# A hybrid encoder on one core: attention traced as generators between weight groups, gate jobs moved late, the first two odd jobs in one loop

## The chip, the cores and the metric

The kernel runs on one core of a Trainium2 chip. The metric is device time in microseconds of one execution, the median of several runs; a profile shows one further execution, instruction by instruction.

## The reference, cut to what matters

Sequence 256, width 2048, 16 heads of 128, batch 1, all float32. One even layer, one odd layer, a final RMS norm.

```python
# even layer
u = rms_norm(h, ln_even_g)
qa, ka, va, qb, kb, vb, gate = split(u @ w_in_even)           # 2048 x 6656
ya = gqa_attention(rope(rms_norm(qa)), rope(rms_norm(ka)), va)      # 8 heads (A), 2 key/value heads
yb = diff_attention(qb1, qb2, kb1, kb2, vb, lam, slopes)            # 8 heads (B), two softmaxes each
yb = rms_norm(yb, b_subln_g) * (1 - lambda_init)
h = h + (concat(ya, yb) * silu(gate)) @ w_out_even
# odd layer
qc, kc, vc, gate = split(rms_norm(h, ln_odd_g) @ w_in_odd)     # 2048 x 8192
yc = dilated_window_attention_mix(qc, kc, vc)                       # 16 heads (C)
h = h + (yc * silu(gate)) @ w_out_odd
return rms_norm(h, final_norm_g)
```

## The kernel before

**Weights.** Almost all of TensorE's work is the four projections. They are cut into jobs of 512 output columns. A job has 8 weight groups (`wgroup`, L135) of 1024 values per partition. SP loads a group into `raw` (three buffers), ACT rounds it to `hi` (L151), DVE takes the rest, `lo` (L152); `hi` and `lo` have three buffers each. A product is three matmuls (`mm3`, L157, its lines L159 to L161): hi by hi, hi by lo, lo by hi. A group is 12 matmuls of 512 columns: two token tiles, two slices of the contraction, three products. The activation side (`u`, `y`) is also kept as hi and lo. A job's two sums lie in two of the four `acc` banks until ACT or DVE has read them.

**Order.** The program is traced once, in Python; a scheduler then lays the instructions in each engine's queue by its own estimate of when they are ready, with trace order as priority. The weight splits L151 and L152 are traced at high priority. After that each queue runs in order on the chip.

**Moving a tile to the other layout.** `turned` (L246) transposes 128x512 in 32x32 blocks on DVE (two instructions, L250), and four DMAs of POOL's queue (L254) move the blocks between partitions into a tile `pt`. The reader of `pt` is most often a split (hi on ACT, lo on DVE) ahead of a matmul. `turned_pe` (L257) does the same with four TensorE transposes (L262) and is used for the last group of B heads alone.

**Even layer (L537 to L559).** Job kv, then for each of two groups of heads: q of A, gate of A, gate of B, q of B, k of B, v of B. Behind the gate of A the four A heads are traced (scores L335 to L337, softmax L343 to L348, `turned`, `weights`, `weighted_v` L361, which multiplies by the gate at L367 and splits into `y`). Behind k of B the softmaxes of four B heads are traced (`softmax_b`, L390), behind v the rest (`pair_b`, L411, with the gate in L430). So the last B heads of the second group stand at the very end of the layer, behind its last projection job.

**Output projections.** `jobs_out` (L182) runs the first two jobs in one loop: weight groups 0 to 5 of both, then groups 6 and 7 of both; groups 6 and 7 read `y[12]` to `y[15]`, which are finished last. After each even output job DVE adds the residual, and `turned` with `times_turned` builds the next layer's `u`.

**Odd layer (L578 to L602).** Four times: gate, q, k, v; the softmaxes of four heads behind k, the weighted sums behind v.

Of the kernel before, what the change touches and what calls it, by code (L numbers as in the profile page):

```python
# [17 lines left out]
P = 128  # L18
# [46 lines left out]
def job_columns(name):  # L65

    if name == "even":
        cols = [(A_KV0, 512)]
        for c in (0, 512):
            cols += [(b + c, 512) for b in (0, GATE_E, GATE_E + 1024, B_Q0, B_K0, B_V0)]  # L70
        return cols
    if name == "odd":
        return [(b * D + c, 512) for c in range(0, D, 512) for b in (3, 0, 1, 2)]
    return list(CHUNKS_E if name == "out_even" else CHUNKS)
# [19 lines left out]
def trunk(ctx, tc, x, xt, w_even, w_oe, w_odd, w_oo, gain_cols, rows, final_g, rope_c, geo_c, out):  # L94
# [24 lines left out]
    ones = work.tile([P, 512], F32, tag="x", name="ones", bufs=2)[:, :P]  # L119
    G.memset(ones, 1.0)  # L120
    ident = const.tile([P, P], F32, name="ident")
    make_identity(nc, ident)
# [10 lines left out]
    loads, splits = [], []  # L133

    def wgroup(wb, c0, wd, kg, into=None, pieces=1, beside=None):  # L135
        w, where = wb
        kn = 1024 // wd
        raw = wpool.tile([P, 1024], F32, tag="raw", name="raw", bufs=3)
        if into is None:
            hi = wpool.tile([P, kn, wd], F32R, tag="hi", name="hi")  # L140
            lo = wpool.tile([P, kn, wd], F32R, tag="lo", name="lo")
        else:
            hi, lo = into
        rv = raw.rearrange("p (k c) -> p k c", k=kn)
        n = kn // pieces
        for i in range(pieces):
            ks = slice(i * n, (i + 1) * n)
            cs = slice(i * n * wd, (i + 1) * n * wd)
            loads.append(nc.sync.dma_start(raw[:, cs], w[where[c0] + kg][:, cs]))
            with tc.high_priority():  # L150
                A.activation(hi[:, ks], rv[:, ks], AF.Copy)  # L151
# [3 lines left out]
        return hi, lo  # L155

# [9 lines left out]
    def job_steps(ps, w, c0, wd, a, kgs, beside=None, pieces=lambda kg: 1):  # L166
        kn = 1024 // wd
        for kg in kgs:
            hi, lo = wgroup(w, c0, wd, kg, pieces=pieces(kg), beside=beside)
            for t in range(NT):  # L170
                for kk in range(kn):
                    k = kg * kn + kk
                    ts = slice(t * P, (t + 1) * P)
                    mm3(ps[t], a[k][:, 0, ts], a[k][:, 1, ts], hi[:, kk], lo[:, kk], k == 0, k == NK - 1)

# [6 lines left out]
    def jobs_out(w, chunks, a):  # L182

        (c0, wd), (c1, _) = chunks[:2]
        ps = [job_banks(wd) for _ in range(2)]
        for kgs in (range(6), range(6, 8)):
            for p, c in zip(ps, (c0, c1)):
                job_steps(p, w, c, wd, a, kgs)
        for i, (c, wd) in enumerate(chunks):
            yield i, slice(c, c + wd), ps[i] if i < 2 else job_t(w, c, wd, a)  # L190
# [4 lines left out]
    u = [ug[k // UG][:, k % UG] for k in range(NK)]  # L195

    def make_u(k, src, gain):

        A.activation(u[k][:, 0], src, AF.Copy, scale=gain)  # L199
        V.scalar_tensor_tensor(u[k][:, 1], src, gain, f(u[k][:, 0]), op0=ALU.mult, op1=ALU.subtract)  # L200
# [45 lines left out]
    def turned(src):  # L246

        x = work.tile([P, 4, 4, 32], F32, tag="x", name="x", bufs=2)
# [7 lines left out]

    def turned_pe(src):  # L257

        ps = att.tile([P, 512], F32, tag="att", name="tp").rearrange("p (n k) -> p n k", n=4)
        for j in range(2):  # L260
            for t in range(NT):
                T.transpose(ps[:, 2 * j + t], src[:, t, j * P:(j + 1) * P], ident)  # L262
        return ps.rearrange("p n (a c) -> p n a c", a=4)
# [18 lines left out]
    def pair_t(z, pair, tag, bufs=2):  # L282

        ps = turned(cols(z, pair))
# [6 lines left out]
    def pair_q64(z, pair):  # L291
        ps = turned(cols(z, pair))
# [7 lines left out]
    def pair_k64(z, pair):  # L300
        ps = turned(cols(z, pair))
# [59 lines left out]
    def weighted_v(h, p, v, vs, gate):  # L361
        ph, pl = weights(p)
        o = bank()[:, :S]
# [46 lines left out]
    def pair_b(h, ps, v, zg, turned):  # L410

        os = []
        ss = small.tile([P, 8], F32, tag="ss8", name="ss4", bufs=2)[:, :2 * NT]
        for j in range(2):
            ph, pl = weights(ps[j])
# [10 lines left out]
        yt = stile()  # L426
        for j in range(2):
            c = slice(j * HD, j * HD + HD)
            for t in range(NT):
                V.scalar_tensor_tensor(yt[:, t, c], os[j][:, t], r[:, 2 * j + t:2 * j + t + 1], zg[:, t, c], op0=ALU.mult,  # L430
                                       op1=ALU.mult)
        yt = turned(yt)
        for j in range(2):
            y[h + j] = acts.tile([P, 2, S], F32R, tag="y", name="y")
            times_turned(y[h + j][:, 0], y[h + j][:, 1], yt[:, 2 * j:2 * j + 2], gsub[:, 0:1])
# [100 lines left out]
    k_a = pair_t(tok_heads(ps_kv, 1, 2), 0, "ka", 1)  # L536
    for g in range(2):  # L537
        c = 512 * g
        zq = tok_heads(job_t(w_even, c, 512, u) if g else ps_q0, 0, 4)
        qs = [pair_t(zq, pair, "q") for pair in range(2)]  # L540
        zg = gate_t(job_t(w_even, GATE_E + c, 512, u), rh)
        for pair in range(2):
            gate = turned(cols(zg, pair))
            for j in range(2):
                p = softmax_a(qs[pair][:, :, j], k_a[:, :, g])
                weighted_v(4 * g + 2 * pair + j, p, v_a[:, 0], slice(g * HD, g * HD + HD), gate[:, 2 * j:2 * j + 2])
        zg = gate_t(job_t(w_even, GATE_E + 1024 + c, 512, u), rh)
        zq = evac_t(job_t(w_even, B_Q0 + c, 512, u), rs)
        qs = [pair_q64(zq, pair) for pair in range(2)]
        zk = evac_t(job_t(w_even, B_K0 + c, 512, u), rstd)  # L550
        v = v_tile()
        ps = []
        for pair in range(2):
            kh, kl = pair_k64(zk, pair)
            for j in range(2):
                ps.append(softmax_b(4 * g + 2 * pair + j, qs[pair][:, :, j], kh[:, :, j], kl[:, :, j]))
        evac_v(v, job_t(w_even, B_V0 + c, 512, u), rstd)
        for pair in range(2):
            pair_b(8 + 4 * g + 2 * pair, ps[2 * pair:2 * pair + 2], v[:, pair], cols(zg, pair), turned_pe if g else turned)  # L559


    y_even = list(y)
    un = [acts.tile([P, UG, 2, S], F32R, tag="u", name="u", bufs=NK // UG) for _ in range(NK // UG)]
    u = [un[k // UG][:, k % UG] for k in range(NK)]
    parts_o = small.tile([P, NT, 4], F32, tag="parts4", name="parts4", bufs=1)
    for i, cs, ps in jobs_out(w_oe, CHUNKS_E, y_even):
        for t in range(NT):
            V.tensor_add(tok[:, t, cs], tok[:, t, cs], ps[t])
        for k in range(cs.start // P, cs.stop // P, 2):
            xk = turned(tok[:, :, k * P:k * P + S])  # L570
            for m in range(2):
                src, gain = xk[:, 2 * m:2 * m + 2], gcol[:, NK + k + m:NK + k + m + 1]
                times_turned(u[k + m][:, 0], u[k + m][:, 1], src, gain)
        for t in range(NT):
            square_sum(parts_o[:, t, i:i + 1], tok[:, t, cs])


    for g in range(4):  # L578
# [4 lines left out]
        zg = gate_t(ps, rh)  # L583
        gates = [turned(cols(zg, pair)) for pair in range(2)]
        zq = evac_t(job_t(w_odd, c, 512, u), rs)
        qs = [pair_t(zq, pair, "q") for pair in range(2)]
        zk = evac_t(job_t(w_odd, D + c, 512, u), rstd)
        p = []
        for pair in range(2):
            k = pair_t(zk, pair, "k")  # L590
            p += [softmax_c(4 * g + 2 * pair + j, qs[pair][:, :, j], k[:, :, j]) for j in range(2)]
        v = v_tile()
        evac_v(v, job_t(w_odd, 2 * D + c, 512, u), rstd)
        for pair in range(2):
            for j in range(2):
                weighted_v(4 * g + 2 * pair + j, p[2 * pair + j], v[:, pair], slice(j * HD, j * HD + HD),
                           gates[pair][:, 2 * j:2 * j + 2])
# [80 lines left out]
```

## Time and profile before

| | us |
|---|---|
| median of 3 runs (lowest, highest) | 950.54 (948.35, 951.49) |
| profiled execution, its own time | 952.57 |
| span of its trace | 950.8 |
| PE busy (matmul) | 890.5 (94% of the span) |
| DVE busy | 650.4 (68%) |
| ACT busy | 523.7 (55%) |
| POOL busy | 257.1 (27%) |
| mean granted TensorE clock | 0.964 of full speed |

How to read it: matmuls are pipelined, so a busy PE is not a PE at its peak; what counts is the distance from one matmul's start to the next. The granted clock is full (2.4 GHz) in most of the span and falls to half (1.2 GHz) in parts of one stretch near the middle. Idle time of DVE, ACT and POOL costs nothing as long as PE goes on.

### The profile page before, as it was taken

How to read it: one execution, taken by the hardware profiler on the slowest of the kernel's cores; microseconds unless marked ns; L12 is line 12 of the kernel's file. 1: busy time of each engine (PE TensorE's matmuls, PEld its weight loads, DVE VectorE, ACT ScalarE, POOL GpSimd, SP SyncE). 2: the span in 40 equal slices, each digit the busy share in tenths (PEclk: the TensorE clock that was granted, in tenths of full speed). 3: DMA queues.
4: the chain of work that ended last, by engine and by line, in shares of the span. 5: the costliest groups of instructions: out<-in, count | busy, mean ns of one | idle time of the engine just before them, and what ended most of it. 6: DMA issues, size and time to landing. Idle time of an engine off the chain costs nothing.

```text
span 950.8 us, 12189 instructions
## 1 busy us (share of the span) xinstructions
PE 890.5 (94%) x4124; PEld 742.3 (78%) x4124; DVE 650.4 (68%) x937; ACT 523.7 (55%) x842; POOL 257.1 (27%) x395
## 2 busy tenths in 40 slices
PE   9999999999999666279999999999999999999896
PEld 7788888888888555267888888888888888888686
DVE  6688656787786557537776666767776776676564
ACT  6756655677555436525554455655554565455442
POOL 0023102132231232423121233424332433251200
PEclk9999999999999779569999999999999999999999
DMA  8867666564566434115766656665576657665553
GB/s 295 296 218 236 218 200 210 189 220 166 189 225 216 135 89 166 34 55 165 237 221 218 220 188 212 222 213 194 191 243 214 202 183 226 228 208 183 175 199 133
DMA packets 57662, 186.16 MB, mean 196 GB/s; under 512 B 10688, under 2 KB 11456, under 8 KB 57600
## 3 DMA queue, kind: packets, MB, share of 16 engines
q1 hardware_dynamic: 46656, 162.57, 50.9%
q0 software_dynamic: 10944, 22.83, 8.1%
q8 instruction: 32, 0.52, 0.2%
q14 instruction: 30, 0.25, 0.1%
HBM read 161.50 MB, written 2.10 MB: 172 GB/s over the span
## 4 chain that ended last, share of the span: by engine, by line
PE 56%; DVE 2%; ACT 2%; issue 2%; DMA 2%; POOL 1%; POOLq 0%; DVEq 0%; ACTq 0%
PE acc_t L159 18%; PE acc_t L160 17%; PE acc_t L161 17%; DMA pt<-x 2%; POOL pt L254 1%; PE bank L160 1%; ACT s L346 1%; PE bank L161 1%; PE bank L159 1%; DVE x L250 0%; PE bank L337 0%; PE bank L336 0%; PE bank L335 0%; ACT hi L151 0%; DVE s L381 0%
## 5 line engine op out<-in xcount | busy, mean ns | idle before, releaser
L152 DVE TENSOR_TENSOR lo<-raw,hi 128x1024 fp32r<-128x1024 f32 (+1 forms) x294 | 360.1, 1226 | 197.3 <-ACT hi L151 196.6
L151 ACT ACTIVATE hi<-raw 128x1024 fp32r<-128x1024 f32 (+1 forms) x294 | 309.0, 1053 | 279.0 <-PE acc_t L161 228.0
L160 PE MATMUL acc_t<-lo,u 128*128 128x512 f32 x928 | 360.5, 390 | 0.5 <-DVE lo L152 0.2
L161 PE MATMUL acc_t<-hi,u 128*128 128x512 f32 x928 | 359.9, 390 | 0.0
L159 PE MATMUL acc_t<-hi,u 128*128 128x512 f32 x928 | 330.2, 390 | 0.6 <-ACT u L199 0.6
L254 POOL DMA_DIRECT2D pt<-x x332 | 180.9, 574 | 402.1 <-issue 135.1
L160 PEld LDWEIGHTS acc_t<-lo,u 128*128 128x128 f32 x928 | 174.1, 188 | 37.6 <-DVE lo L152 2.4
L159 PEld LDWEIGHTS acc_t<-hi,u 128*128 128x128 f32 x928 | 174.0, 188 | 37.3 <-ACT u L199 1.6
L161 PEld LDWEIGHTS acc_t<-hi,u 128*128 128x128 f32 x928 | 174.3, 188 | 35.2
L159 PE MATMUL acc_t<-hi,y 128*128 128x512 f32 (+1 forms) x256 | 95.4, 397 | 6.0 <-ACT y L225 4.6
L160 PE MATMUL acc_t<-lo,y 128*128 128x512 f32 (+1 forms) x256 | 100.1, 393 | 0.4 <-DVE lo L152 0.4
L161 PE MATMUL acc_t<-hi,y 128*128 128x512 f32 (+1 forms) x256 | 95.4, 388 | 0.0
L386 POOL TENSOR_SCALAR bias<-geo 128x512 f32<-128x512 f32 x24 | 40.3, 1681 | 166.1 <-DVE s L381 160.6
L159 PEld LDWEIGHTS acc_t<-hi,y 128*128 128x128 f32 x256 | 50.6, 198 | 18.5 <-ACT y L225 6.2
L160 PEld LDWEIGHTS acc_t<-lo,y 128*128 128x128 f32 x256 | 50.6, 198 | 10.1 <-DVE lo L152 1.1
L161 PEld LDWEIGHTS acc_t<-hi,y 128*128 128x128 f32 x256 | 50.3, 197 | 9.4
L346 ACT ACTIVATE s<-s,nm 128x256 f32<-128x256 f32 x64 | 31.9, 499 | 32.3 <-DVE nm L343 31.4
L250 DVE STREAM_TRANSPOSE x<-z 128x256 f32<-128x256 f32 x82 | 46.9, 611 | 3.4 <-DMA pt<-x 3.3
L250 DVE STREAM_TRANSPOSE x<-s 128x256 f32<-128x256 f32 x68 | 39.7, 620 | 3.8 <-ACT s L376 3.4
L225 ACT ACTIVATE ph<-pt 128x512 fp32r<-128x512 f32 x32 | 19.9, 621 | 26.6 <-DMA pt<-x 26.6
L232 ACT ACTIVATE z<-acc_t,rstd 128x512 f32<-128x512 f32 x40 | 26.9, 680 | 7.4 <-PE acc_t L161 5.7
L226 DVE TENSOR_TENSOR pl<-pt,ph 128x512 fp32r<-128x512 f32 x32 | 21.7, 677 | 13.5 <-ACT ph L225 13.5
(140 smaller groups left out, 704.4 us busy)
## 6 DMA issues: line engine op xcount, KB each, us to landing
raw<-in_w_in_odd SPq DMA_DIRECT2D x128, 512.0 KB, 4.1
raw<-in_w_in_even SPq DMA_DIRECT2D x102, 512.0 KB, 4.1
pt<-x POOLq DMA_DIRECT2D x332, 64.0 KB, 3.3
raw<-in_w_out_even SPq DMA_DIRECT2D x32, 512.0 KB, 3.3
raw<-in_w_out_odd SPq DMA_DIRECT2D x32, 512.0 KB, 3.6
tok<-in_x SPq DMA_DIRECT2D x4, 512.0 KB, 8.1
xk<-in_xt SPq DMA_DIRECT2D x6, 256.0 KB, 5.5
raw<-in_w_in_even SPq DMA_DIRECT2D x4, 256.0 KB, 4.4
```

The costliest lines, as they stand in the source:

```text
L151: A.activation(hi[:, ks], rv[:, ks], AF.Copy)
L152: splits.append(V.tensor_sub(lo[:, ks], rv[:, ks], f(hi[:, ks])))
L159: T.matmul(ps, ah, bh, start=start, stop=False)
L160: T.matmul(ps, ah, bl, start=False, stop=False)
L161: T.matmul(ps, al, bh, start=False, stop=stop)
L225: A.activation(hi, src, AF.Copy)
L226: V.tensor_sub(lo, src, f(hi))
L232: A.activation(z[:, t], ps[t], AF.Copy, scale=r[:, t:t + 1])
L250: V.transpose(x[:, :, 2 * m:2 * m + 2].rearrange("p b t c -> p t b c"), src[:, :, m * P:(m + 1) * P].rearrange("p t (r b) -> p t b r", b=4))
L254: G.dma_start(dst[:, a].rearrange("p n c -> p (n c)"), x[32 * a:32 * a + 32].rearrange("r b n c -> r (b n c)"))
L346: A.activation(e[:, t], s[:, t], AF.Exp, bias=nm[:, t:t + 1], accum_out=den[:, t:t + 1])
L386: G.tensor_scalar_mul(b, geo[:, 0], -slope)
```

## The change

1. `tick()` is called after each weight group. Attention steps become generators (`spawn`): each runs up to a `yield n` and goes on n weight groups later. So the pieces of the attention of one job are traced between the weight groups of the next jobs, at distances written by hand (6 to 10 groups from a `turned` to the reader of its tile).
2. `behind()` ties the readers of a moved tile, on ACT and on DVE, behind the split of the weight group that was traced last.
3. Even jobs in a new order: kv, q of A twice, then q, k, v of B, a gate, and again q, k, v of B, and three gates. The gates are no longer needed for the attention: A heads leave an ungated sum in `o` (a copy of ACT), B heads a normalised one in `yt` (ACT); `finish` and `finish_b` multiply by the gate later. The weight blocks lie in memory in the new order.
4. Odd jobs: q, k, v, gate for the first two groups, then q, k, v of the third and fourth, then the last two gates. The first q and k share a loop (`two_jobs`) as the output jobs do.
5. `turned_pe` and the identity are gone; tag `x`, which `turned` writes, has four buffers in place of two. `u` of the next layer is made by `task_u`, five groups after its `turned`.

```diff
-        cols = [(A_KV0, 512)]
-        for c in (0, 512):
-            cols += [(b + c, 512) for b in (0, GATE_E, GATE_E + 1024, B_Q0, B_K0, B_V0)]
-        return cols
+        return [(c, 512) for c in (A_KV0, 0, 512, B_Q0, B_K0, B_V0, GATE_E, B_Q0 + 512, B_K0 + 512, B_V0 + 512,
+                                   GATE_E + 1024, GATE_E + 512, GATE_E + 1536)]
...
+        quads = [(b * D + c, 512) for c in range(0, D, 512) for b in (0, 1, 2, 3)]
+        return quads[:11] + quads[12:15] + quads[11:12] + quads[15:]
...
+    tasks, now = [], [0]
+    def spawn(steps, delay=0):
+        tasks.append([now[0] + delay, steps])
+    def tick():
+        now[0] += 1
+        for task in list(tasks):
+            if task[0] <= now[0]:
+                try:
+                    task[0] = now[0] + next(task[1])
+                except StopIteration:
+                    tasks.remove(task)
...
+    @contextmanager
+    def behind():
+        with tc.issue_after(firsts[-1].ins), tc.issue_after(splits[-1].ins):
+            yield
...
+                    advance(lambda: a[k] is not None)
                     mm3(ps[t], a[k][:, 0, ts], a[k][:, 1, ts], hi[:, kk], lo[:, kk], k == 0, k == NK - 1)
+            tick()
...
+    def weighted_v(o, p, key):
+        yield 6
+        with behind():
+            ph, pl = weights(p)
+        yield 1
+        yield from until(lambda: key in values)
+        v, vs = values[key]
+        ps = bank()[:, :S]
         for kt in range(NT):
-            mm3(o, v[:, kt, 0, vs], v[:, kt, 1, vs], ph[:, kt], pl[:, kt], kt == 0, kt == NT - 1)
-        yf = work.tile([P, S], F32, tag="yf", name="yf")
-        V.tensor_mul(row_quarters(yf), row_quarters(o), gate)
-        y[h] = acts.tile([P, 2, S], F32R, tag="y", name="y")
-        split(y[h][:, 0], y[h][:, 1], yf)
+            mm3(ps, v[:, kt, 0, vs], v[:, kt, 1, vs], ph[:, kt], pl[:, kt], kt == 0, kt == NT - 1)
+        A.copy(o, ps)
+    def finish(h, o, gate):
+        gate = turned(gate)
+        yield 6
+        with behind():
+            V.tensor_mul(quarters(o), quarters(o), gate)
+        for j in range(2):
+            y[h + j] = acts.tile([P, 2, S], F32R, tag="y", name="y")
+            split(y[h + j][:, 0], y[h + j][:, 1], o[:, j])
...
+    def pair_b(i, q, kh, kl, outs):
+        ps = []
+        for j in range(2):
+            ps.append(softmax_b(i + j, q[:, :, j], kh[:, :, j], kl[:, :, j]))
+            yield 2
+        yield 4
+        yield from until(lambda: ("b", i) in values)
...
-                V.scalar_tensor_tensor(yt[:, t, c], os[j][:, t], r[:, 2 * j + t:2 * j + t + 1], zg[:, t, c], op0=ALU.mult,
-                                       op1=ALU.mult)
-        yt = turned(yt)
+                A.activation(yt[:, t, j * HD:(j + 1) * HD], os[j][:, t], AF.Copy, scale=r[:, 2 * j + t:2 * j + t + 1])
+        outs[i // 2] = yt
+    def finish_b(h, i, outs, gate):
+        yield from until(lambda: outs[i] is not None)
+        V.tensor_mul(outs[i], outs[i], gate)
+        yt = turned(outs[i])
+        yield 6
...
+    def task_bk(g, z, qs):
+        ts = [turned(cols(z, pair)) for pair in range(2)]
+        yield 7
+        for pair in range(2):
+            with behind():
+                kh, kl = pair_k64(ts[pair])
+            yield 1
+            spawn(pair_b(4 * g + 2 * pair, qs[pair], kh, kl, ob))
+            yield 4
...
     for g in range(2):
         c = 512 * g
+        spawn(task_bq(evac_t(job_t(w_even, B_Q0 + c, 512, u), rs), qs))
+        spawn(task_bk(g, evac_t(job_t(w_even, B_K0 + c, 512, u), rstd), qs))
+        ps = job_t(w_even, B_V0 + c, 512, u)
...
+        if g:
+            zg = gates(1024)
+            for pair in range(2):
+                spawn(finish_b(8 + 2 * pair, pair, ob, cols(zg, pair)))
+        zg = gates(c)
+        for pair in range(2):
+            spawn(finish(4 * g + 2 * pair, oa[2 * g + pair], cols(zg, pair)))
+    zg = gates(1536)
+    for pair in range(2):
+        spawn(finish_b(12 + 2 * pair, 2 + pair, ob, cols(zg, pair)))
...
     for g in range(4):
         c = 512 * g
-        ps = job_t(w_odd, 3 * D + c, 512, u)
         if g == 0:
+            ps_q, ps_k = two_jobs(w_odd, c, D + c, u)
             rstd, rs, rh = token_stats(parts_o, 1.0 / math.sqrt(HD))
...
+        if g < 2:
+            gates(g)
+    gates(2)
+    gates(3)
```

## Rows read from the trace of the kernel before

**Rows 1.** Stretches of the span: busy us (instructions) of each engine, granted clock.
```profile
core 0: us, PE busy (x) PEld busy (x) DVE busy (x) ACT busy (x) POOL busy (x), PEclk, DMA share, GB/s
220.00:300.00 80.00, 80.00 (x389) 67.40 (x388) 64.63 (x102) 48.52 (x89) 25.12 (x37) 1.00 0.60 198
300.00:440.00 140.00, 93.29 (x389) 75.41 (x388) 80.77 (x139) 63.38 (x137) 40.73 (x63) 0.78 0.32 102
0.00:431.00 431.00, 382.69 (x1722) 316.58 (x1723) 294.68 (x461) 244.43 (x429) 105.85 (x166) 0.93 0.56 185
440.00:860.00 420.00, 420.00 (x1926) 350.37 (x1925) 295.76 (x388) 235.15 (x339) 136.16 (x205) 1.00 0.65 214
874.00:896.00 22.00, 18.70 (x78) 14.88 (x77) 11.75 (x19) 9.43 (x17) 6.53 (x12) 0.92 0.66 215
```

**Rows 2.** Chain that ended last, about 440 us: start, us, what.
```profile
438.32 0.45 PE acc_t L159 x2
441.04 0.45 PE acc_t L159 x2
```

**Rows 3.** Timeline of PE: start, us, engine, line, operation, tiles, shape.
```profile
307.52 0.28 PE L335 MATMUL bank<-ka,q 128*128 128x256 f32 x1
308.72 0.28 PE L161 MATMUL bank<-ph,va 128*128 128x256 f32 x1
```

**Rows 4.** PE's instructions by form in 300 to 440: count, busy, mean, idle before.
```profile
L160 PE MATMUL acc_t<-lo,y 128*128 128x512 f32 x75 | 32.9, 439 | 0.4 <-DVE lo L152 0.4
L398 PE MATMUL bank<-kh,q 128*128 128x256 f32 x16 | 5.2, 369 | 17.6 <-ACT kh L307 17.6
L160 PE MATMUL bank<-v,ph 128*128 128x128 f32 x16 | 5.1, 319 | 0.0
L160 PE MATMUL acc_t<-lo,u 128*128 128x512 f32 x12 | 4.7, 389 | 0.0
L159 PE MATMUL bank<-ph,va 128*128 128x256 f32 x8 | 3.3, 415 | 12.4 <-ACT ph L225 12.4
L262 PE MATMUL tp<-ident,s 128*128 128x128 f32 x8 | 2.6, 453 | 11.3 <-DVE s L430 11.3
L337 PE MATMUL bank<-ka,q 128*128 128x256 f32 x6 | 2.2, 371 | 0.0
```

**Rows 5.** Chain that ended last, 370 to 412 and 872 to 900.
```profile
377.06 3.81 DMA pt<-x
...
882.07 5.88 DMA pt<-x
```

**Rows 6.** PE's instructions by form in 874 to 896.
```profile
L160 PE MATMUL bank<-pl,v 128*128 128x256 f32 x4 | 1.6, 390 | 0.3 <-DVE pl L226 0.3
```

**Rows 7.** All waits: engine, line, waited for; us in total, times, longest.
```profile
ACT hi L151 <- PE acc_t L161: 228.0, 178, 6.8
ACT ph L225 <- DMA pt<-x: 26.6, 13, 5.4
PE acc_t L159 <- ACT y L225: 4.6, 4, 1.5
```

**Rows 8.** Groups of instructions over the span: count, busy us, mean ns.
```profile
L152 DVE TENSOR_TENSOR lo<-raw,hi 128x1024 fp32r<-128x1024 f32 (+1 forms) x294 | 360.1, 1226 | 197.3 <-ACT hi L151 196.6
L250 DVE STREAM_TRANSPOSE x<-s 128x256 f32<-128x256 f32 x68 | 39.7, 620 | 3.8 <-ACT s L376 3.4
L343 DVE TENSOR_REDUCE nm<-s 128x2 f32<-128x512 f32 x32 | 21.5, 681 | 0.4
L381 DVE TENSOR_TENSOR s<-bank,bias 128x512 f32<-128x512 f32 x32 | 21.5, 680 | 6.8 <-PE bank L399 4.7 <-POOL bias L388 0.7 <-POOL bias L386 0.6
L346 ACT ACTIVATE s<-bank,nm 128x256 f32<-128x256 f32 x16 | 7.4, 471 | 9.4 <-DVE nm L343 9.4
```

**Rows 9.** Line L254, POOL's DMA issues: ns min/median/max; then DMA to landing.
```profile
L254 POOL DMA_DIRECT2D pt<-x x332: 534/569/752, 57.9 to 882.1; - x166
...
DMA to landing us min/median/max: 2.0/3.3/6.7
```

More of the change, by code (lines that the diff above doesn't have):

```diff
@@ L1 @@
 import math
-from contextlib import ExitStack, nullcontext
+from contextlib import ExitStack, contextmanager
 import numpy as np
@@ L8 @@
 from concourse import mybir
-from concourse.masks import make_identity
 F32 = mybir.dt.float32
@@ L130, in trunk @@
         T.matmul(idle[:, :P], ones, ones, start=True, stop=True)
-    loads, splits = [], []
+    loads, firsts, splits = [], [], []
     def wgroup(wb, c0, wd, kg, into=None, pieces=1, beside=None):
@@ L194, in trunk @@
     ug = [acts.tile([P, UG, 2, S], F32R, tag="u", name="u", bufs=NK // UG) for _ in range(NK // UG)]
-    u = [ug[k // UG][:, k % UG] for k in range(NK)]
+    u = [None] * NK
     def make_u(k, src, gain):
+        u[k] = ug[k // UG][:, k % UG]
         A.activation(u[k][:, 0], src, AF.Copy, scale=gain)
@@ L246, in turned @@
     def turned(src):
-        x = work.tile([P, 4, 4, 32], F32, tag="x", name="x", bufs=2)
+        x = work.tile([P, 4, 4, 32], F32, tag="x", name="x", bufs=4)
         for m in range(2):
@@ L535, in trunk, with task_ka, head_a, task_a @@
     evac_v(v_a, ps_kv, rstd, 256)
-    k_a = pair_t(tok_heads(ps_kv, 1, 2), 0, "ka", 1)
+    keys_a = []
+    def task_ka(z):
+        ps = turned(z)
+        yield 8
+        with behind():
+            keys_a.append(pair_t(ps, "ka", 1))
+    oa, ob = [out_pair() for _ in range(4)], [None] * 4
+    def head_a(o, q, k, key):
+        yield from weighted_v(o, softmax_a(q, k), key)
+    def task_a(g, z):
+        qs = [turned(cols(z, pair)) for pair in range(2)]
+        yield 10
+        for pair in range(2):
+            with behind():
+                q = pair_t(qs[pair], "q")
+            yield 1
+            for j in range(2):
+                spawn(head_a(oa[2 * g + pair][:, j], q[:, :, j], keys_a[0][:, :, g], ("a", g)), 2 * j)
+            yield 3
@@ new lines, in task_bq @@
+    def task_bq(z, qs):
+        ts = [turned(cols(z, pair)) for pair in range(2)]
+        yield 8
+        for pair in range(2):
+            with behind():
+                qs.append(pair_q64(ts[pair]))
+    def task_bk(g, z, qs):
+        ts = [turned(cols(z, pair)) for pair in range(2)]
+        yield 7
+        for pair in range(2):
+            with behind():
+                kh, kl = pair_k64(ts[pair])
+            yield 1
+            spawn(pair_b(4 * g + 2 * pair, qs[pair], kh, kl, ob))
+            yield 4
@@ L537, in trunk, with gates @@
+    for g in range(2):
+        values["a", g] = v_a[:, 0], slice(g * HD, g * HD + HD)
+    spawn(task_ka(tok_heads(ps_kv, 1, 2)))
+    spawn(task_a(0, tok_heads(ps_q0, 0, 4)))
+    spawn(task_a(1, tok_heads(job_t(w_even, 512, 512, u), 0, 4)))
+    def gates(c):
+        return gate_t(job_t(w_even, GATE_E + c, 512, u), rh)
     for g in range(2):
         c = 512 * g
-        zq = tok_heads(job_t(w_even, c, 512, u) if g else ps_q0, 0, 4)
-        qs = [pair_t(zq, pair, "q") for pair in range(2)]
@@ L562, in trunk @@
[L562 to L565 removed]
+        qs = []
+        spawn(task_bq(evac_t(job_t(w_even, B_Q0 + c, 512, u), rs), qs))
+        spawn(task_bk(g, evac_t(job_t(w_even, B_K0 + c, 512, u), rstd), qs))
+        ps = job_t(w_even, B_V0 + c, 512, u)
+        v = v_tile()
+        evac_v(v, ps, rstd)
@@ new lines, in trunk @@
+        for pair in range(2):
+            values["b", 4 * g + 2 * pair] = v[:, pair]
+        if g:
[3 more added lines that the diff above has]
+        zg = gates(c)
+        for pair in range(2):
+            spawn(finish(4 * g + 2 * pair, oa[2 * g + pair], cols(zg, pair)))
+    zg = gates(1536)
+    for pair in range(2):
+        spawn(finish_b(12 + 2 * pair, 2 + pair, ob, cols(zg, pair)))
+    y_even = y
@@ new lines, in trunk, with task_u @@
+    ug = [acts.tile([P, UG, 2, S], F32R, tag="u", name="u", bufs=NK // UG) for _ in range(NK // UG)]
+    parts_o = small.tile([P, NT, 4], F32, tag="parts4", name="parts4", bufs=1)
+    def task_u(cs):
+        ks = range(cs.start // P, cs.stop // P, 2)
+        xs = [turned(tok[:, :, k * P:k * P + S]) for k in ks]
+        yield 5
+        for k, x in zip(ks, xs):
+            for m in range(2):
+                un[k + m] = ug[(k + m) // UG][:, (k + m) % UG]
+                with behind():
+                    times_turned(un[k + m][:, 0], un[k + m][:, 1], x[:, 2 * m:2 * m + 2],
+                                 gcol[:, NK + k + m:NK + k + m + 1])
@@ L568, in trunk @@
             V.tensor_add(tok[:, t, cs], tok[:, t, cs], ps[t])
[L569 to L573, printed above, removed]
+        spawn(task_u(cs))
         for t in range(NT):
             square_sum(parts_o[:, t, i:i + 1], tok[:, t, cs])
+    u = un
+    y = [None] * NK
@@ new lines, in trunk, with gates, head_c, task_q @@
+    oc = []
+    def gates(g):
+        zg = gate_t(job_t(w_odd, 3 * D + 512 * g, 512, u), rh)
+        for pair in range(2):
+            spawn(finish(4 * g + 2 * pair, oc[2 * g + pair], cols(zg, pair)))
+    def head_c(h, o, q, k):
+        yield from weighted_v(o, softmax_c(h, q, k), ("c", h))
+    def task_q(z, qs):
+        ts = [turned(cols(z, pair)) for pair in range(2)]
+        yield 7
+        for pair in range(2):
+            with behind():
+                qs.append(pair_t(ts[pair], "q"))
@@ L578, in trunk, with task_k @@
+    def task_k(g, z, qs):
+        ts = [turned(cols(z, pair)) for pair in range(2)]
+        yield 6
+        for pair in range(2):
+            with behind():
+                k = pair_t(ts[pair], "k")
+            yield 1
+            for j in range(2):
+                h = 4 * g + 2 * pair + j
+                spawn(head_c(h, oc[2 * g + pair][:, j], qs[pair][:, :, j], k[:, :, j]), 2 * j)
+            yield 3
     for g in range(4):
         c = 512 * g
-        ps = job_t(w_odd, 3 * D + c, 512, u)
@@ L592, in trunk @@
-        v = v_tile()
[L593 to L597, printed above, removed]
+        else:
+            ps_q, ps_k = job_t(w_odd, c, 512, u), None
+        qs = []
+        oc += [out_pair() for _ in range(2)]
+        spawn(task_q(evac_t(ps_q, rs), qs))
+        spawn(task_k(g, evac_t(ps_k or job_t(w_odd, D + c, 512, u), rstd), qs), 1)
@@ L600, in trunk @@
+        ps = job_t(w_odd, 2 * D + c, 512, u)
+        v = v_tile()
+        evac_v(v, ps, rstd)
+        for i in range(4):
+            values["c", 4 * g + i] = v[:, i // 2], slice(i % 2 * HD, i % 2 * HD + HD)
+        if g < 2:
+            gates(g)
+    gates(2)
+    gates(3)
     parts = small.tile([P, NT, 5], F32, tag="parts5", name="parts5", bufs=1)
```

82 lines of the change are left out of this document (27 added, 55 removed).

## The prediction, made before the changed kernel ran

> **What bounds the kernel now.** I read the stretches of the span first, for PE's instruction count and the granted clock; then the chain that ended last, for the pace of an undisturbed matmul; then the waits and the groups of instructions, for what would be next.
>
> From 440 to 860 PE is busy without a gap at full clock [rows 1]. Its pace there is that of the weight groups: the chain shows the same matmul pair of one group and of the next 2.72 us apart, 438.32 and 441.04 [rows 2]. A group is 12 matmuls of 512 columns, so one is 2.72 / 12 = 0.2267 us. ACT rounds each group and then waits for PE to give a buffer back, 228.0 us in 178 waits [rows 7]: the splits run ahead, DVE and ACT are not the bound there. So the odd layer has nothing to give except at its end.
>
> From 300 to 440 it is different. The stretch holds 389 PE instructions, as many as the 80 us from 220 to 300, but takes 140 us, and the clock's mean falls to 0.78 [rows 1]. What PE waits for there is attention of the second head group: `ph` of the A heads (12.4 us), `kh` of the last B pair (17.6 us), the scaled tile of the PE transpose (11.3 us) [rows 4]. The chain shows what these waits are made of: landings of moved tiles, such as 3.81 us at 377.06 [rows 5], each followed by a split, scores, a softmax and the next move. No projection work is left to run beside it but the first output jobs, and their last groups read just these heads. The same at the end of the odd layer, from 874 to 896: 78 instructions in 22 us [rows 1], with a landing of 5.88 us in the chain [rows 5].
>
> **The sum: what the stretches would take at full pace.** From 300 to 440 the forms are: 512 columns, 75 and 12 for each of the three products (two records of one line are missing there, so 259 found); 256 columns, 16 each of two lines (L398, L399), 8 and 6 each of three lines, so 74; 128 columns, 16 each of three lines, and 8 transposes, so 56 [rows 4]. Ten steps of 256 columns take 308.72 - 307.52 = 1.20 us, 0.12 each [rows 3]; I take the same for 128 columns, an upper bound. 259 x 0.2267 + (74 + 56) x 0.12 = 58.7 + 15.6 = 74.3 us. Lost: 140 - 74.3 = 65.7 us. It includes the half clock after each gap, which goes with the gap.
>
> From 874 to 896: 12 of the 78 have 256 columns, 4 each of three lines [rows 6]. 66 x 0.2267 + 12 x 0.12 = 16.4 us; lost: 5.6 us.
>
> **The change, part by part.**
>
> *Order and generators, even layer.* The last projection job is now a gate, and two more gates stand ahead of it. The B heads of the second group are traced from 7 groups after job k of B on, and end some 24 groups after it, at the end of the second of the three gates. Behind the last job there remain only evacuation, tanh, a product, one move and one split. For that, the output loop offers 12 groups, 12 x 2.72 = 32.6 us, ahead of the first reader of `y[12]`. The move itself: two transposes at 0.620 [rows 8], four issues at 0.569, landing 3.3 [rows 9], together 6.8 us; with the longest values 1.24 + 3.0 + 6.7 = 10.9 us. With six groups (16.3 us) of written delay the split is still well ahead. So the whole 65.7 us go, and the 8 TensorE transposes with them (1.0 us): -66.7.
>
> *Gates last, odd layer.* The last projection job is a gate here too, and nothing but a product stands behind it: -5.6. If the cover failed, it would cost again what 874 to 896 cost.
>
> *First odd jobs in one loop.* The border of the layers lies behind 440, and from there to 860 PE loses nothing [rows 1]; twice the cover for `u[12]` to `u[15]` is worth 0 here.
>
> *What is added.* 24 copies of a weighted sum on ACT, at most the 0.471 of another PSUM read of that width [rows 8], 11.3 us, and 16 scalings of half that width, at most 7.5 us. DVE loses as many products and gains one of 512 columns for each pair. Eight more DMAs on POOL, 8 x 0.569 = 4.6 us. All of it lies beside PE: with the loss gone, the work from 0 to 431 stands in 431 - 66.7 = 364 us, and then ACT has (244.4 + 18.8) / 364 = 72%, POOL (105.9 + 4.6) / 364 = 30%, DVE 294.7 / 364 = 81% [rows 1]. DVE is the one to look at. But from 220 to 300 it had 64.63 / 80 = 81% and PE lost nothing [rows 1]. So I take 0 for the additions; the other end is the first rival.
>
> *New waits.* Each copy on ACT waits for a weighted sum of PE, and the next L151 is queued behind it. PE needs that split only when the buffered groups are used up, two groups or 5.4 us later. `behind` makes a reader of a moved tile wait behind the newest split, on both engines, and what follows in the queue waits with it. In the trace of before ACT waited 13 times for `pt` of `ph`, 26.6 us in all, at most 5.4 [rows 7]: about the slack of the buffers. With the written delays these waits should vanish. I price them at 0, with the second rival as the other end.
>
> *Joints.* Where an output loop reads its first late `y`, PE waited 4.6 us in 4 places, at most 1.5 [rows 7]. Those in the middle and end stretches are in the sums above; new joints can cost between 0 and 4.6; I take half, +2.3.
>
> Profiled execution: 952.57 - 66.7 - 5.6 + 2.3 = 882.6. The median of before lies 2.0 below its profiled execution, so **880.5** as a median. The start and the tail behind the last matmul stay as they are.
>
> **Rivals.**
>
> *DVE becomes the bound in places* (chance 0.15). For each group of four B heads the softmaxes are traced within 8 weight groups. On DVE a head takes 2 x (0.680 + 0.681) + 2 x 0.620 = 3.96 us [rows 8] without its smaller steps; four heads 15.8, eight splits at 1.226 [rows 8] 9.8, together 25.6 us. PE needs 21.8 + 4 x 8 x 0.12 = 25.6 us for the same. So DVE is full before the small steps, the key splits, the gate products and the moves of neighbouring jobs. If those add a quarter, 6.4 us, at each of three dense places (two B groups, and the rotary work of q of A, now two jobs in a row), and no buffer takes it up, 19 us come back: 878 + 19 = 897, some more with half clock. For it: the count. Against it: the splits have priority, a late softmax delays only itself, and the average is that of a stretch without loss.
>
> *Moved tiles late in the queue: slower than before* (0.04). The diff has 97 `behind` blocks when their loops are run out. If a tile took longer than its delay (6 groups, 16.3 us; 5 groups, 13.6, for `u`) plus the two buffered groups, each block would hold up the splits behind it and PE with them. It decides at about 16.3 + 5.4 = 22 us from transpose to landing, where the rows give 7 to 11, or 13 with two tiles in a row on POOL's queue. To eat up the 72 us, 0.75 us at each block are enough; at 1 us each the time would be 878 + 97 = 975. The rule behind it is in the Trainium skill, "TensorE: Matmul & The Clock Gate", section on the array's architectural detail: ACT and DVE take their queues in strict order, and only PE pulls weight loads ahead. By that rule one late tile stops every split behind it, which speaks against `behind`; the ACT waits on moved tiles named above agree with it. A second rule would lengthen the landing: the Trainium skill, "DMA: Bandwidth & Descriptors", section "SWDGE vs HWDGE vs iDMA", says that DVE can lock GpSimd out of the memory in which it writes its descriptors. The trace does not bear it out: the issues took 534 to 752 ns over the whole span [rows 9], dense DVE stretches included. The sum without it is the one above; with it, this rival.
>
> *Half the tail stays* (0.06). Trace order is only a priority. If the scheduler still puts the second group's B heads late, or the yields are too long for the three gates to cover, about half of 66.7 stays: 878 + 33 = 911.
>
> *It doesn't do what it says* (0.03). The gaps only move to the new joints, for instance because moved tiles find no free slot in their pool. I count at most 21 of its 22 slots in use in trace order, so little speaks for it; the time would be about 950.
>
> **How the numbers follow.** The forecast has 0.72. Its own range is 873 to 889: downwards from 878.2 without joints, less the spread of the three runs (3.1 us) and some 2 us for paces read to 0.01 us over 130 small matmuls; upwards with all of the joints and one dense place. The range with 8 in 10 takes in the first rival: **873 to 900**. A difference within 0.3% (2.9 us) can't be told from none here. Faster: 0.72 + 0.15 + 0.06 = 0.93; same: 0.03; slower: 0.04.
>
> **What would show it.** Right: full granted clock in every stretch up to the tail; no PE gap above 1.5 us between 50 us and the tail; PE's count in any 20 us of the even layer at the full-pace level; ACT's waits on `pt` near 0; the wait of L151 for PE still the largest. Wrong: PE waiting for `lo` (DVE is the bound), L151 behind a late `ph` or `y`, or a gap with `kh`, `ph` or `y` as releaser just ahead of the output loops. What would break the sum most is a scheduler order on PE in which an attention matmul stands ahead of its input on the chip: a gap of the landing's size, followed by half clock, for each.

## The result and the profile after

| | before | after |
|---|---|---|
| median, us (lowest, highest) | 949.79 (948.35, 951.49) | 880.29 (880.15, 880.41) |
| profiled execution / its span | 952.57 / 950.8 | 880.24 / 878.5 |
| PE busy | 890.5 (94%) | 868.3 (99%) |
| DVE / ACT / POOL busy | 68% / 55% / 27% | 74% / 61% / 31% |
| mean granted TensorE clock | 0.964 | 0.997 |

The ratio is 0.9268, 95% interval 0.925 to 0.9285. The forecast was 880.5. PE's busy time fell by 22 us although its work is the same but for eight transposes: matmuls at half clock count as busy for longer (from 300 to 440 the `lo` by `y` product took 439 ns as a mean before [rows 4], 389 after).

The stretches of the kernel after, in the form of [rows 1] (busy us and instructions of each engine, granted clock, DMA):

```profile
core 0: us, PE busy (x) PEld busy (x) DVE busy (x) ACT busy (x) POOL busy (x), PEclk, DMA share, GB/s
60.00:300.00 240.00, 239.50 (x1170) 201.73 (x1169) 204.60 (x310) 173.99 (x332) 93.77 (x137) 1.00 0.61 203
180.00:220.00 40.00, 40.00 (x203) 33.95 (x202) 38.34 (x66) 30.62 (x67) 20.71 (x28) 1.00 0.61 197
300.00:440.00 140.00, 140.00 (x625) 116.13 (x625) 99.73 (x151) 75.54 (x115) 31.27 (x56) 1.00 0.67 221
```

From 300 to 440 PE now runs 625 instructions where it ran 389 [rows 1], at full clock. Of them 612 have 512 columns and 13 have 128, which at the pace of [rows 2, 3] is 140.3 us: no loss is left. All that PE still waits for, in the whole span (engine, line, waited for; us in total, times, longest):

```profile
PE idle L126 <- POOL nhalf L120: 1.0, 1, 1.0
PE acc_t L187 <- DVE lo L148: 0.7, 2, 0.5
PE acc_t L186 <- ACT u L232: 0.3, 1, 0.3
```

No wait for `ph`, `kh` or `y` is left [rows 4]. ACT's waits for moved tiles and for PE, to be set beside [rows 7]:

```profile
ACT hi L147 <- PE acc_t L188: 196.7, 155, 2.7
ACT ph L258 <- DMA pt<-x: 13.5, 11, 2.7
```

The splits still run ahead of PE. In this span the difference is 950.8 - 878.5 = 72.3 us, which is the prediction's 66.7 + 5.6. By place, with the first matmul of the odd layer and the last of the kernel, before and then after:

```profile
476.33 0.62 PE L159 MATMUL acc_t<-hi,u 128*128 128x512 f32 x2
942.46 0.28 PE L161 MATMUL acc_l<-u,y 128*128 128x256 f32 x1
```

```profile
409.75 0.62 PE L186 MATMUL acc_t<-hi,u 128*128 128x512 f32 x2
870.14 0.28 PE L188 MATMUL acc_l<-u,y 128*128 128x256 f32 x1
```

The odd layer starts 66.6 us earlier, and takes 460.4 us from there to the last matmul in place of 466.1: 5.7 less. The place and the size were right. The experiments ask for the cause.

### The profile page after: what moved, and what is told of

The parts are those of the page before. It is cut to its first block, busy times and chain, and to the rows that moved or that the text cites. A ratio compares the mean times of both kernels' runs of the same rounds, so it can differ in the third digit from the quotient of the medians.

```text
span 878.5 us, 12205 instructions
## 1 busy us (share of the span) xinstructions
PE 868.3 (99%) x4116; PEld 728.4 (83%) x4116; DVE 649.0 (74%) x917; ACT 531.8 (61%) x882; POOL 271.0 (31%) x401
## 4 chain that ended last, share of the span: by engine, by line
PE 94%; DMA 2%; DVE 1%; ACT 1%; issue 1%; SPq 0%; POOLq 0%; POOL 0%; DVEq 0%; ACTq 0%
PE acc_t L187 29%; PE acc_t L188 29%; PE acc_t L186 29%; PE bank L187 1%; DMA raw<-in_w_in_even 1%; PE bank L188 1%; PE bank L186 1%; DMA tok<-in_x 1%; PE bank L359 1%; PE bank L358 1%; PE bank L357 1%; DVE lo L148 0%; PE bank L438 0%; PE bank L437 0%; ACT hi L147 0%
## 5 line engine op out<-in xcount | busy, mean ns | idle before, releaser
L287 POOL DMA_DIRECT2D pt<-x x340 | 185.4, 593 | 331.0 <-ACT hi L147 109.4
L188 PE MATMUL acc_t<-hi,y 128*128 128x512 f32 (+1 forms) x256 | 96.1, 376 | 0.0
L187 PE MATMUL acc_t<-lo,y 128*128 128x512 f32 (+1 forms) x256 | 96.1, 376 | 0.0
L186 PE MATMUL acc_t<-hi,y 128*128 128x512 f32 (+1 forms) x256 | 87.0, 376 | 0.0
L425 POOL TENSOR_SCALAR bias<-geo 128x512 f32<-128x512 f32 x24 | 45.7, 1905 | 131.8 <-DVE s L420 124.2
L187 PEld LDWEIGHTS acc_t<-lo,y 128*128 128x128 f32 x256 | 48.2, 188 | 8.8
L186 PEld LDWEIGHTS acc_t<-hi,y 128*128 128x128 f32 x256 | 48.1, 188 | 8.8
L188 PEld LDWEIGHTS acc_t<-hi,y 128*128 128x128 f32 x256 | 48.2, 188 | 8.6
L283 DVE STREAM_TRANSPOSE x<-s 128x256 f32<-128x256 f32 x64 | 37.1, 621 | 6.7 <-ACT s L495 5.9
L259 DVE TENSOR_TENSOR pl<-pt,ph 128x512 fp32r<-128x512 f32 x32 | 26.0, 812 | 2.1 <-ACT ph L258 2.1
```

The lines of the kernel that those rows point to most:

```text
L186: T.matmul(ps, ah, bh, start=start, stop=False)
L187: T.matmul(ps, ah, bl, start=False, stop=False)
L188: T.matmul(ps, al, bh, start=False, stop=stop)
L259: V.tensor_sub(lo, src, f(hi))
L283: V.transpose(x[:, :, 2 * m:2 * m + 2].rearrange("p b t c -> p t b c"), src[:, :, m * P:(m + 1) * P].rearrange("p t (r b) -> p t b r", b=4))
L287: G.dma_start(dst[:, a].rearrange("p n c -> p (n c)"), x[32 * a:32 * a + 32].rearrange("r b n c -> r (b n c)"))
```

## The experiments

**What carries the gain: ties, delays or order.** Theory at this point: the new job order and the written delays carry it; `behind()` is an insurance. First `behind()` is made empty.

```diff
     def behind():
-        with tc.issue_after(firsts[-1].ins), tc.issue_after(splits[-1].ins):
-            yield
+        yield
```

> The changed kernel with behind() made empty: readers of moved tiles are no longer tied behind the newest weight split; job order and written delays stay. Theory (job order and delays carry the gain, behind() is only an insurance): 880 to 884 us, PE without gaps from 50 us to the tail. Rival (behind() carries it, since ACT and DVE take their queues in order and a late tile stops the splits behind it): 890 to 930 us, PE gaps released by DVE lo or ACT hi in the even layer.

Measured: 881.29 us, ratio to before 0.9278 (0.9264 to 0.9292), against 0.9268 (0.925 to 0.9285) with the ties. They are worth nothing that can be told here.

Then the delays are taken out: a spawned step runs through at once, in trace order, unless a value is missing.

```diff
     def spawn(steps, delay=0):
-        tasks.append([now[0] + delay, steps])
+        for step in steps:
+            if step is None:
+                tasks.append(steps)
+                return
...
     def until(ready):
         while not ready():
-            yield 1
+            yield None
```

> The changed kernel with every written delay taken out: a spawned step runs to its end at once, except where it needs a value that a later job makes; behind() and the job order stay. Theory in its narrow form (the job order alone carries the gain): 880 to 890 us. Rival (the delays carry it): the readers stand behind a split before their tile has landed, ACT waits for pt more than 60 us in all (13.5 us in the changed kernel), and 900 to 950 us.

> Job order alone: delays and behind() both taken out. Theory in its narrow form (the job order alone carries the gain): 880 to 890 us, like the run with behind() and no delays. Rival (generators carry it): 920 to 950 us, gaps as in the kernel before.

Measured: 954.2 us with the ties, 955.01 without; ratios 1.0054 (1.0036 to 1.0073) and 1.0053 (1.0036 to 1.007). So the new job order alone gives nothing; it is even 0.5% slower than the old. The theory in its narrow form has fallen. The rivals said 900 to 950 and 920 to 950: both are passed by 4 to 5 us, and the mechanism that the first of them names is not there. ACT waited for `pt` of `ph` only 14.4 us, not over 60. PE's largest waits with delays out and ties in:

```profile
PE acc_t L186 <- ACT y L258: 21.4, 2, 19.9
PE bank L186 <- ACT ph L258: 18.7, 5, 7.6
PE acc_t L186 <- ACT z L265: 6.4, 1, 6.4
```

The heads are late again, with three gate jobs traced behind them. Being traced early did not make them early.

The other half: everything as in the changed kernel, but k of the second B group is the last projection job.

```diff
-    ... B_Q0 + 512, B_K0 + 512, B_V0 + 512, GATE_E + 1024, GATE_E + 512, GATE_E + 1536
+    ... B_Q0 + 512, B_V0 + 512, GATE_E + 1024, GATE_E + 512, GATE_E + 1536, B_K0 + 512
```

(The list is cut at its start; the calls of the jobs follow the same order.)

> Generators, delays and behind() as in the changed kernel, but the k job of the second B group is the last even projection job, behind the three gates and v; so scores, softmaxes and weighted sums of four heads again stand behind the last projection job. Theory (what counts is that no attention stands there): the kernel loses a good part of the 65.7 us again, 905 to 950 us, gaps with kh, ph or y as releaser just ahead of the output loops. Rival (the way of tracing carries the gain): 880 to 890 us.

Measured: 910.58 us, 0.9587 (0.9573 to 0.9601). Order matters: 30 us, once the heads are traced with delays. Without the delays the order gives nothing; without the order the delays still give 39 of the 69.5 us.

**Why the heads were late.** The trace of before has the answer at a place where nothing is lost yet, and which the prediction did not look at. Three moments of PE's timeline before, one A head each (start, us, engine, line, operation, tiles, shape):

```profile
104.86 0.28 PE L159 MATMUL bank<-ph,va 128*128 128x256 f32 x1
104.97 0.28 PE L335 MATMUL bank<-ka,q 128*128 128x256 f32 x1
...
122.64 0.28 PE L159 MATMUL bank<-ph,va 128*128 128x256 f32 x1
122.75 0.28 PE L335 MATMUL bank<-ka,q 128*128 128x256 f32 x1
...
140.42 0.28 PE L159 MATMUL bank<-ph,va 128*128 128x256 f32 x1
140.53 0.28 PE L335 MATMUL bank<-ka,q 128*128 128x256 f32 x1
```

The first score of a head (L335) starts 0.11 us after the first matmul of the weighted sum of the head before it (L159), each time, and the distance from head to head is 17.78 us. The scores need only `q` and `k`; the last split of `q` ends at 89.0 us. What both take is a bank: scores and sums share the tag `att` of one pool. The new theory: the next head's bank is given out only after the bank that was traced ahead of it, that of the sum, which waits for its moved tile. So the heads run one at a time, whatever stands around them; the moved tiles `pt` and the `y` share a tag too. The written delays break that chain because a head's sum is traced seven groups behind its scores, so that other heads' scores come first. It would explain the run without delays too: there the first scores of successive A heads start at 105.7, 123.5 and 141.3 us, 17.8 apart. Test: leave the kernel before as it is and give the sums banks of their own.

```diff
-    att = ctx.enter_context(tc.tile_pool(name="att", bufs=4, space=PSUM))
+    att = ctx.enter_context(tc.tile_pool(name="att", bufs=2, space=PSUM))
...
+    def sum_bank():
+        return att.tile([P, 512], F32, tag="sum", name="sum")
...
-        o = bank()[:, :S]
+        o = sum_bank()[:, :S]
...
```

(The sums of the B heads take `sum_bank()` in the same way. Two banks for scores and two for sums are the four that they shared before.)

> The kernel before with one edit: the weighted sums take their PSUM bank from a tag of their own (two banks for scores, two for sums) and no longer from the tag of the scores; job order and in-place tracing stay. New theory (in the kernel before, heads run one after another, 17.6 us each, because a bank for the scores of head j+1 can only be given out after the bank for the sum of head j, which waits for its moved tile; the written delays undo just that): the scores of the next heads move ahead, and part of the 65.7 us goes: 920 to 942 us. Rival (the loss comes from the job order, whatever the tags): 946 to 953 us.

> The kernel before with own tags for the sums' banks and for the moved tiles pt (6 slots; 16 are left for y), so that neither waits for the tile that an earlier head allocates last. New theory: more of the loss goes than with the banks alone, 905 to 930 us. Rival (job order): 946 to 953 us.

The second of the two has besides:

```diff
-    acts = ctx.enter_context(tc.tile_pool(name="acts", bufs=22))
+    acts = ctx.enter_context(tc.tile_pool(name="acts", bufs=16))
...
-        dst = acts.tile([P, 4, 4, 32], F32, tag="y", name="pt")
+        dst = acts.tile([P, 4, 4, 32], F32, tag="pt", name="pt", bufs=6)
```

Measured: 935.88 us, 0.9858 (0.9835 to 0.9881), and 907.13 us, 0.9553 (0.9535 to 0.9571). Both lie in the new theory's ranges, the rival's 946 to 953 is out. So the old order gives 43 us with two small edits. How many score matmuls of one line PE had done between 84 and 104 us (two make one head), for the kernel before, with the sums' own tag, with both own tags, and for the kernel after, in this order:

```profile
L335 PE MATMUL bank<-ka,q 128*128 128x256 f32 x2 | 0.6, 280 | 0.0
```

```profile
L338 PE MATMUL bank<-ka,q 128*128 128x256 f32 x8 | 2.2, 281 | 0.0
```

```profile
L338 PE MATMUL bank<-ka,q 128*128 128x256 f32 x8 | 2.2, 281 | 0.0
```

```profile
L357 PE MATMUL bank<-ka,q 128*128 128x256 f32 x8 | 2.2, 281 | 0.0
```

One head against four: a tag of their own lets the scores go ahead just as the delays do. That shared tags chained the heads is shown; that it comes from the order in which the slots are given out is how we explain it, and no run separates it from other effects of a tag.

The same in the new job order, still without delays, first with the sums' tag, then with both (`pt` has 5 slots, `y` 17):

> The changed kernel's job order traced in place without delays (954.2 us), and an own PSUM tag for the weighted sums. New theory (order and unchained heads together make the gain, the generators being one way to unchain them): 885 to 915 us. Rival (only the written delays place the readers rightly): above 935 us.

> The changed kernel's job order traced in place, without written delays, with own tags for the sums' banks (2) and the moved tiles (5 slots, 17 left for y). Theory (new job order plus heads that are not chained by a shared tag are the whole gain; generators and delays are one way to unchain them): 879 to 888 us, no PE gap over 1.5 us behind 50 us. Rival (written delays are needed in themselves): above 895 us.

Measured: 928.7 us, 0.9782 (0.9762 to 0.9802), just short of "above 935" of the rival and above the theory's 885 to 915; and 899.21 us, 0.9471 (0.9455 to 0.9486), above the theory's 879 to 888 and inside the rival's "above 895". Both miss upwards, and by its time the second speaks for the rival, that the written delays are needed in themselves. It has only a single long gap left, at the first late reader in the output loop:

```profile
329.32 0.39 PE L188 MATMUL acc_t<-hi,y 128*128 128x512 f32 x1
343.92 0.80 PE L186 MATMUL acc_t<-hi,y 128*128 128x512 f32 x1 [14.21 <-ACT y L258]
344.51 0.63 PE L187 MATMUL acc_t<-lo,y 128*128 128x512 f32 x1
344.94 0.63 PE L186 MATMUL acc_t<-hi,y 128*128 128x512 f32 x1
```

The matmuls behind the gap start 0.43 us apart in place of 0.2267: half clock (granted 0.50 from 343.9 to 346.6), which brings the gap's 14.2 us to about 16, an estimate from these starts. It is a gated A head that comes late. ACT's rows show where the lateness begins: its gate left the banks (`z`) at 298.4 to 300.5, but the first tanh of any of the three gates starts at 321.45, just behind a square of the last B heads' sums, and its own at 326.55:

```profile
298.35 0.67 ACT L265 ACTIVATE z<-acc_t,rstd 128x512 f32<-128x512 f32 x1
...
321.05 0.28 ACT L244 ACTIVATE sq<-sum 128x128 f32<-128x128 f32 x1
...
321.45 0.63 ACT L273 ACTIVATE th<-z 128x512 f32<-128x512 f32 x1
...
326.55 0.65 ACT L273 ACTIVATE th<-z 128x512 f32<-128x512 f32 x1
```

In the kernel after, the same gate's tanh starts at 300.90, 3.1 us behind its `z`. The squares (`sq`) and the tanh (`th`) share a tag of one buffer in the program, so this may be a third chain of the same kind; no run gave them tags of their own. Without the gap the run would stand near 883, by the estimate above. So order and unchained heads give 50 of the 69.5 us without generators. How much of the other 19 is one more shared tag, and how much only delays can give, is open.

| | heads chained | own tags, no delays | delays |
|---|---|---|---|
| attention behind the last projection job | 950.2 | 907.1 | 910.6 (k last) |
| gates last in the even layer | 954.2 | 899.2 | 880.3 |

The upper row holds two orders: the old one in its first two cells, in which only the sums of the last heads stand behind the last job, and k last in the third, in which their scores stand there too. In the old order the delays were not tried.

**The odd layer.** v last in each group, so that the weighted sums of four heads stand behind the last projection job; and, apart from it, the first two odd jobs one after the other.

```diff
-        quads = [(b * D + c, 512) for c in range(0, D, 512) for b in (0, 1, 2, 3)]
-        return quads[:11] + quads[12:15] + quads[11:12] + quads[15:]
+        return [(b * D + c, 512) for c in range(0, D, 512) for b in (0, 1, 3, 2)]
...
```

(The gate job is called ahead of v, and its product waits until both heads of its pair have their sums.)

> The changed kernel with the odd jobs as q, k, gate, v in each of the four groups, so that the last projection job is v and the weighted sums of four heads, their gates and splits stand behind it; generators, delays, behind() and the shared first loop stay. Theory of the prediction (gates last is worth the 5.6 us at the end of the odd layer): 884 to 889 us, a PE gap ahead of or in the last output loop. Rival (with the delays, 12 groups of the output loop cover that too): 879 to 882 us.

```diff
-            ps_q, ps_k = two_jobs(w_odd, c, D + c, u)
+            ps_q, ps_k = job_t(w_odd, c, 512, u), None
```

> The changed kernel with the first odd q and k jobs one after the other in place of the shared loop. Prediction (the shared loop is worth 0, six groups cover the move of u): 879.5 to 882 us. Rival (the cover of six groups is too short now that u is read five groups behind its move): 884 to 895 us, a PE gap released by ACT u or DVE u at about 420 us.

Measured: 880.88 us, 0.9279 (0.9262 to 0.9296), and 881.23 us, 0.9279 (0.9264 to 0.9295), against 0.9268 (0.925 to 0.9285). Neither differs from the changed kernel by more than the intervals. The prediction's -5.6 for "gates last" in the odd layer is not the order's alone. First matmul of the odd layer and last of the kernel, in the new order without delays (954.2 us) and then with v last:

```profile
483.01 0.61 PE L186 MATMUL acc_t<-hi,u 128*128 128x512 f32 x2
944.08 0.28 PE L188 MATMUL acc_l<-u,y 128*128 128x256 f32 x1
```

```profile
410.14 0.62 PE L185 MATMUL acc_t<-hi,u 128*128 128x512 f32 x2
870.79 0.28 PE L187 MATMUL acc_l<-u,y 128*128 128x256 f32 x1
```

That is 461.1 and 460.7 us, against 466.1 before and 460.4 after. Gates last without delays, or delays without gates last: either takes most of the loss away. What the new order without delays loses is all in the even layer, which ends 6.7 us later than before.

**How far DVE is.** Extra reductions on DVE behind each even weight split but those of the first two jobs (`extra` is a tile of one column that nothing reads).

```diff
+            if wb is w_even and c0 not in (A_KV0, 0):
+                V.reduce_sum(extra, tok[:, 0, :256], axis=AX.X)
```

> The changed kernel with one more DVE reduction of 256 columns behind the split of each weight group of the even projection jobs but the first two (88 of them, about 0.4 us each, 35 us in all); it is extra work. First rival of the prediction (DVE is the next bound; from 60 to 300 it is busy 85% in the changed kernel, and this makes it about 99%): 885 to 900 us, PE gaps released by DVE lo. Against it (the buffers take it up): 880 to 884 us.

> The same with 512 columns (88 of about 0.65 us, 57 us in all; DVE from 60 to 300 would need about 107%). Rival of the prediction (DVE next): 895 to 925 us. If DVE's work can slide into the stretch of the output jobs without holding up the splits: 880 to 890 us.

Measured: 890.57 us, 0.938 (0.9366 to 0.9394), and 906.65 us, 0.9548 (0.9533 to 0.9563). The added work as its group in the smaller load (operation, tiles and shapes, count | busy us, mean ns | idle before them), and in the larger, whose reductions read 512 columns in place of 256:

```profile
L151 DVE TENSOR_REDUCE extra<-tok 128x1 f32<-128x256 f32 x88 | 36.3, 412 | 0.6
```

```profile
L151 DVE TENSOR_REDUCE extra<-tok 128x1 f32<-128x512 f32 x88 | 59.5, 676 | 0.3
```

The stretch from 60 to 300 in the smaller and in the larger load, in the columns of the first fence of the section on the result (PE, PEld, DVE, ACT, POOL, clock, DMA):

```profile
60.00:300.00 240.00, 239.86 (x1161) 201.79 (x1160) 218.12 (x358) 169.03 (x314) 85.23 (x127) 1.00 0.63 203
```

```profile
60.00:300.00 240.00, 238.84 (x1142) 199.95 (x1141) 227.28 (x344) 162.96 (x289) 78.23 (x117) 1.00 0.64 202
```

36.3 us of work cost 10.3 us, 59.5 us cost 26.4. The times fit the rival's ranges, the place does not: DVE reaches 91% and 95%, not the 99% and 107% that were expected, PE is busy all through the stretch, and PE's waits for `lo` stay below 2 us in both. The bill comes at the output loops, where PE waits for `y`; in the larger one it first waits for `ph` and `pl` of the last heads (PE's waits for `u` in the smaller load, 2.2 us, lie in the first 9 us, ahead of the first added reduction):

```profile
PE acc_t L189 <- ACT y L261: 5.3, 1, 5.3
```

```profile
PE acc_t L189 <- ACT y L261: 9.2, 1, 9.2
PE bank L189 <- ACT ph L261: 4.9, 2, 3.5
PE bank L191 <- DVE pl L262: 4.7, 2, 2.4
```

The splits stay in time; what slides is the attention, until it runs out of projection work to hide behind. 26 us of the smaller load (36.3 - 10.3) and 33 us of the larger (59.5 - 26.4) cost nothing; the larger also put late heads into the output loops.

## Why the prediction was right, and where it was not

*The sum* was right: 65.7 + 1.0 + 5.6 = 72.3 us off the profiled execution, measured 952.57 - 880.24 = 72.33. Counting matmuls at the undisturbed pace gave the loss in each stretch, half clock included, without having to follow each gap.

*Two terms were wrong and cancelled, which is luck.* The joints were priced at +2.3; the kernel after has no wait for `y` at all. And the median of before lay 2.0 below its profiled execution; the kernel after has 880.29 against 880.24, no such offset. Without either term the forecast would have been 880.3.

*The cause was named in part.* The step that does not hold as it was reasoned is "Order and generators, even layer": it read from the waits between 300 and 440 that attention stands behind the last projection job, and took moving jobs there to be the cure. With that order and no delays the time is 954.2. What stood there were the last of heads that run one at a time from 85 us on, 17.78 us each at first. The row that would have told it is not among PE's waits, because PE had projection work in the meantime; it is the distance between the heads' scores. The delays unchain the heads, as tags of their own do; the order adds 30 us to that with delays, and about 8 with own tags (907.1 to 899.2), where the late gate takes back some 16.

*Gates last in the odd layer*, -5.6: the loss is gone, but the term is not the order's alone; with the delays, v last gives 880.88. *The first odd jobs in one loop*, 0: right, 881.23 without. *New waits and `behind()`*, 0: right, 881.29 without; it was no harm and no help, and the rival built on late tiles had nothing to decide, since with delays in place ACT waits for `ph` no more than 2.7 us at a time. The rule that it leaned on, strict order in ACT's and DVE's queues (the Trainium skill, "TensorE: Matmul & The Clock Gate", section on the array's architectural detail), is neither borne out nor refuted by these runs. Nor do the steady issue times, 534 to 752 ns [rows 9], test the second rule that this rival names, on descriptors: the Trainium skill ("DMA: Bandwidth & Descriptors", section "SWDGE vs HWDGE vs iDMA") binds it to DVE's 2-port perf mode, and no row shows DVE in it.

*The additions*, 0: right. From 180 to 220 DVE is busy 38.34 of 40 us and PE loses nothing. The first rival had the next bound right, and its mechanism wrong: a loaded DVE holds up the heads, not the splits.

## What to carry to other kernels

When a pipeline stage comes late, look at the distance between its repeats where nothing is lost yet: equal distances while the inputs lie ready point to a chain, and a chain is broken where its links share something (here a tag of a pool, 43 us by two small edits), not where the stall shows. Moving work behind a chain that is not broken gains nothing (954 against 950, all of the loss in the even layer). And for a bound engine at a steady pace, instructions times pace against elapsed time gives the loss of a stretch, clock drops included, more surely than the sum of its gaps: from 300 to 440 PE stood idle for 140 - 93.3 = 46.7 us, and the loss by the sum was 65.7.

## What the runs showed of the hardware beside that

A split `pl` on DVE (two inputs in SBUF, 128x512) takes 0.684 us as a median in both kernels, but its mean rose from 677 to 812 ns. Two of those behind it, with what POOL did at the time (start, us, engine, line, operation, tiles, shapes):

```profile
593.68 2.57 DVE L259 TENSOR_TENSOR pl<-pt,ph 128x512 fp32r<-128x512 f32 x1
592.14 2.22 POOL L287 DMA_DIRECT2D pt<-x  x4 [3.72 <-ACT hi L147]
594.33 1.36 POOL L427 TENSOR_TENSOR bias<-bias,geo 128x512 f32<-128x512 f32 x1
...
758.04 2.62 DVE L259 TENSOR_TENSOR pl<-pt,ph 128x512 fp32r<-128x512 f32 x1
756.56 2.22 POOL L287 DMA_DIRECT2D pt<-x  x4 [3.77 <-ACT hi L147]
758.74 1.36 POOL L427 TENSOR_TENSOR bias<-bias,geo 128x512 f32<-128x512 f32 x1
```

In both, DVE's instruction takes nearly four times as long while POOL issues four DMAs and adds a bias. The Trainium skill, "GPSIMD Engine Reference", section "Key points", says that GpSimd shares its SBUF interfaces with VectorE and that DVE instructions with two SBUF inputs contend with it; these two fit that, with 1.9 us each as the price. Not every overlap has it: beside the same POOL addition the weight split `lo`, also with two inputs in SBUF, took 2.19 us at 575.69, where POOL had started 0.2 us earlier, and its usual 1.23 at 694.11, where POOL started 0.4 us later. No run tested it, and PE lost nothing by it.
